# Seven weight tiles' low parts and the pooled channels' low parts, on GpSimd instead of VectorE, during the attention of a hybrid decoder layer

## The chip, the cores and the metric

The kernel runs on one core of a Trainium2 chip. The engines are named as in the profile: PE is TensorE, DVE is VectorE, ACT is ScalarE, POOL is GpSimd, SP is the engine that issues most DMAs. The metric is the device time of one execution in microseconds. The kernel before takes 2540.4 us, the median of three runs from 2538.5 to 2542.72.

## The reference

One layer of a decoder trunk is computed for a prompt of 2048 tokens and for a group of 64 sample tokens, all in float32, with a model width of 1024. Cut to what matters here:

```
h = rmsnorm(x, g_mix);  proj = h @ w_in                 # 1024 -> 512 (q) + 128 (k) + 128 (v) + 512 (u)
p = softmax(q.k / 8 - slope * distance, with a sink)    # 8 heads, window of 128 keys back
attn_o = p @ v
for g, w in enumerate((2, 4, 8, 16)):                   # four groups of 128 channels of u
    d[g] = mean of the last w rows of u[g] - u[g]
pool_o = d @ w_pool * pool_scale
x = x + concat(attn_o, pool_o) @ w_out
x = x + cross_attention(rmsnorm(x), 256 memory tokens) @ w_co
x = x + relu(rmsnorm(x) @ w_up)**2 @ w_down             # hidden 4096
y = rmsnorm(x)
```

The 64 sample tokens have key, value and pooling caches of their own. Caches that the step leaves behind are outputs too.

## The kernel before

**Precision.** PE multiplies a rounded float format (fp32r), so each float32 operand is held as two tiles: `hi`, the value rounded to that format, and `lo`, the rounded rest, `x - hi`. Each product is then three matmuls: hi by hi, hi by lo, lo by hi (`mm3`, and the loop of `dense`, L352 to L354). Making the pair takes a cast to `hi` on ACT and then a subtraction to `lo` on DVE. For weights this is `split`: L118 is the cast of a tile of 128x1024, L119 the subtraction. For activations taken from PSUM it is `rnd` (L97 and L98, with a scale L100 and L101).

**Tokens and weights.** The tokens go through in three superblocks of two token blocks each: 384 and 384, then 256 and 320 (256 of the prompt and the 64 sample tokens), then 384 and 384. The weights are streamed from device memory again for each superblock. The object `S` is this stream: a list of items, each a DMA into one of six `f` tiles and then `split` into two `w` tiles. A pump keeps up to five items ready ahead of their use.

**The stretch around the change.** The input projection has ten column tiles, "in" 0 to 9. Tiles 0 to 5 are keys, values and queries. Tiles 6, 8, 7, 9, in this order, are the four groups of `u`. When the first tiles are through, `mix` interleaves two generators: one runs the projection of the `u` tiles (its three matmuls are L352 to L354), the other runs the attention units. A unit is one block of 128 queries for one of two key heads, in stages: scores on PE (L754) with their maximum on DVE (L755), exponentials on ACT (L766), scaling of the probabilities (L776: one of four heads on DVE, three on POOL), transposes on PE (L785) with `rnd` on ACT and DVE, then the product with v (L802, L803) and its evacuation (L806, L807).

When a `u` tile of one token block is complete, ACT copies it to `uext` (L643), POOL saves or restores the 15 carried columns (L642, L647) and `pool_mix` builds the window sum on POOL by doubling (L672: one addition for window 2, up to four for window 16; for the sample tokens L701). After a delay `pool_fin` turns it into the pooled difference on DVE (L686, sample L706), corrects the first 16 columns on POOL in the first superblock only (L689, L690), casts it to `hi` on ACT (L709) and subtracts to `lo` on DVE (L710). Its output is the second half of the input of the output projection, "wo" 0 to 7, which follows directly in `dense` with L352 to L354 and adds to x in `add_evac` (L970).

**What sets the order.** Python runs the generators and so emits the instructions; a scheduler of the tile framework then reorders them per engine by its own costs, and each engine runs its list strictly in that order. An instruction that waits holds up all behind it on its engine.

Of the kernel before, what the change touches and what calls it, by code (L numbers as in the profile page):

```python
# [12 lines left out]
ALU = mybir.AluOpType  # L13
# [38 lines left out]
def kernel(ctx: ExitStack, tc: tile.TileContext, io, nW=12, nF=6, nT=10):  # L52
    nc = tc.nc
    pool = ctx.enter_context(tc.tile_pool(name="sb", bufs=1))
# [13 lines left out]
    wo_s = drp.tile([8, P, 512], F32, name="wo_s", tag="wo_s")  # L68
# [23 lines left out]
    def f32(ap):  # L92
        return ap.bitcast(F32)
# [9 lines left out]
    def k4(t, n=NB):  # L103
        return t[:, 0:4 * NB].rearrange("p (k n) -> p k n", n=NB)[:, :, 0:n]
# [8 lines left out]
            nc.tensor.matmul(ps, Wh(k), Hl(k), start=False, stop=False)  # L113
            nc.tensor.matmul(ps, Wl(k), Hh(k), start=False, stop=final and i == last)  # L114

    def split(r):
        th, tl = WS.get(), WS.get()
        nc.scalar.copy(th[:], r[:, 0:1024])  # L118
        nc.vector.tensor_tensor(tl[:], r[:, 0:1024], f32(th[:]), ALU.subtract)  # L119
        return th, tl  # L120

    class FB:
# [2 lines left out]
    class Stream:  # L125
# [3 lines left out]
            self.resW = 0  # L129
            self.resF = 0  # L130

        def add(self, key, *raw):
            def fn():
                r = FS.get()
                w = 1024 // len(raw)
                for i, src in enumerate(raw):
                    nc.sync.dma_start(r[:, w * i:w * i + w], src)
                t = split(r)
                FS.put(r)
                return t  # L140

            self.items.append((key, 2, 1, fn))
# [20 lines left out]
    S = Stream()  # L163
# [43 lines left out]
        S.add(("co", c), io["wco"][c])  # L207
    for s in range(3):
        for c in CIN:
            S.add(("in", s, c), io["win"][c])  # L210
            if s == 0 and c in (0, 1):
                for g in range(2):
                    S.add(("wop", 2 * c + g), io["wop"][2 * c + g])
        for c in range(8):
            S.add(("wo", s, c), io["woa"][c], wo_s[c])
        for hf in range(2):
            for kp in range(4):
                S.add(("A", s, hf, kp), a_s[hf, kp])
        for c in BO:
            S.add(("B", s, c), b_s[c])  # L220
        for p in range(NP):
            add_up(s, p)
            pl = (p - 1, p) if p == NP - 1 or s == 1 and p % 2 else () if p == NP - 2 or s == 1 else (p,)
            for t in range(2):
                for i in pl:
                    S.add(("dn", s, i, t), io["wdn"][2 * i + t])
# [332 lines left out]
    def superblock(s, blks, nxt):  # L559
# [120 lines left out]
        def pool_fin(g, bl, src, prev):  # L680
            w = POOLW[g]
            n = bl.np
            ucur = uext[:, g, bl.off + 15:bl.off + 15 + n]
            assert len(dpool.free) == 4
            dt = TS.get()
            nc.vector.scalar_tensor_tensor(dt[:, 0:n], src[:, 0:n], 1.0 / w, ucur, ALU.mult, ALU.subtract)  # L686
            if bl.t0 == 0:
                rc = cst[:, C_RC + 16 * g:C_RC + 16 * g + 16]
                nc.gpsimd.tensor_tensor(dt[:, 0:16], src[:, 0:16], rc, ALU.mult)  # L689
                nc.gpsimd.tensor_tensor(dt[:, 0:16], dt[:, 0:16], ucur[:, 0:16], ALU.subtract)  # L690
            TS.put(prev)
            if bl.ns:
                src = us[:, g, :, 16 - w:23]
                L = 8 + w - 1
                step = 1
                prev = None
                while step < w:
                    t = TS.get()
                    L -= step
                    tv = t[:, 0:8 * L].rearrange("p (b t) -> p b t", t=L)  # L700
                    nc.gpsimd.tensor_tensor(tv, src[:, :, step:step + L], src[:, :, 0:L], ALU.add)  # L701
                    if prev is not None:
                        TS.put(prev)
                    prev, src = t, tv
                    step *= 2
                nc.vector.scalar_tensor_tensor(dt[:, n:n + 64].rearrange("p (b t) -> p b t", t=8), src, 1.0 / w, us[:, g, :, 15:23], ALU.mult, ALU.subtract)  # L706
                TS.put(prev)
            hi, lo = k4(bl.d[0], bl.n)[:, g, :], k4(bl.d[1], bl.n)[:, g, :]
            nc.scalar.copy(hi, dt[:, 0:bl.n])  # L709
            nc.vector.tensor_tensor(lo, dt[:, 0:bl.n], f32(hi), ALU.subtract)  # L710
            TS.put(dt)
            if bl.ns and g == CIN[-1] - 6:
                t = FS.get()
                nc.scalar.copy(t[:, 0:480].rearrange("p (x t) -> p x t", t=15), X0[:, 4 * uw:4 * uw + 736].rearrange("p (x t) -> p x t", t=23)[:, :, 8:23])
                nc.sync.dma_start(io["pools"], t[:, 0:480])
                FS.put(t)
# [566 lines left out]
        def up(p, H=None):  # L1283
# [25 lines left out]
            p6 = prod(wb, (512, 512), "T2")  # L1309
            WS.put(*wb)  # L1310
            r2 = add(TS.get(), p6, r1)
            r4 = add(TS.get(), p5, r2, False)
            w22, *wd = S.next(("up", s, p, 2))
            add(r4, prod(wd, (512, 512), "B22"), r4)
            relu2(H, 1, 0, r4)
            flush()
# [233 lines left out]
```

## Time and profile before

| what | value |
|---|---|
| median of three runs | 2540.4 us |
| profiled execution, its own time | 2537.34 us |
| its span | 2535.3 us |
| PE busy | 98% |
| DVE busy | 73% |
| ACT busy | 43% |
| POOL busy | 7% |

The span runs from the first to the last instruction that the profiler recorded; 2.04 us of the execution's own time lie around it. Where a row has a time and a duration, both are in microseconds from the span's start. A group's row gives the line, engine, operation and tiles, the count after `x`, the busy time, the mean of one in nanoseconds, and then the idle time just ahead of these instructions with what ended it. In a row of the timeline the brackets give the idle time before it and what released it.

### The profile page before, as it was taken

Reading aid. Unit: us, or ns where it says so; the run is one execution under the profiler, and the core shown is the slowest. Engines: PE = TensorE matmul, PEld = TensorE weight load, DVE = VectorE, ACT = ScalarE, POOL = GpSimd, SP = SyncE. Lnnn points to the kernel's source line nnn. Section 1 sums busy time; section 2 is a strip of 40 time slices with the busy share of each in tenths; the row PEclk is TensorE's granted clock in tenths of the full one; section 3 lists DMA queues with packets and bytes.
Section 4 is the critical chain, followed back from the end, with each engine's and each line's share of the span. In section 5 each row is a group of like instructions: output and inputs, shape, how many; then the busy total and the mean of one; then the engine's idle time right before and its main releaser. Section 6 shows DMA issues by size and latency. Waiting matters only on the chain.

```text
span 2535.3 us, 38897 instructions
## 1 busy us (share of the span) xinstructions
PE 2483.3 (98%) x15199; PEld 2368.2 (93%) x15199; DVE 1858.8 (73%) x3687; ACT 1098.6 (43%) x2131; POOL 172.5 (7%) x282
## 2 busy tenths in 40 slices
PE   9899999999999999999999999999999999999998
PEld 9798989999999998996899999989998999999997
DVE  8568537877777788863787877898745877777775
ACT  7666334433333344752544334457534433333332
POOL 0015010000000001411000000003301000000000
PEclk9999999999999999999999999999999999999999
DMA  8833211222222125246522222240412121222211
GB/s 289 270 122 104 92 34 59 67 67 67 67 67 67 61 81 154 82 148 237 212 92 100 76 92 92 88 143 26 142 42 68 42 67 67 67 67 68 67 58 50
DMA packets 92540, 244.73 MB, mean 97 GB/s; under 512 B 16772, under 2 KB 31556, under 8 KB 91204
## 3 DMA queue, kind: packets, MB, share of 16 engines
q1 hardware_dynamic: 92356, 242.25, 28.8%
q8 instruction: 119, 1.95, 0.3%
q14 instruction: 65, 0.53, 0.1%
HBM read 219.53 MB, written 22.69 MB: 96 GB/s over the span
## 4 chain that ended last, share of the span: by engine, by line
PE 78%; DVE 4%; ACT 1%; DMA 1%; POOL 1%; issue 0%; POOLq 0%; DVEq 0%; ACTq 0%
PE mm L112 11%; PE mm L113 11%; PE mm L114 11%; PE aux L112 9%; PE aux L113 9%; PE aux L114 9%; PE mm L352 5%; PE mm L354 5%; PE mm L353 5%; PE aux L754 1%; PE aux L785 1%; DVE x L1371 1%; PE aux L1082 0%; ACT w L118 0%; DVE t L300 0%
## 5 line engine op out<-in xcount | busy, mean ns | idle before, releaser
L118 ACT CAST w<-f 128x1024 fp32r<-128x1024 f32 x378 | 395.6, 1050 | 731.5 <-PE mm L114 366.6
L119 DVE TENSOR_TENSOR w<-f,w 128x1024 fp32r<-128x1024 f32 x378 | 460.4, 1222 | 185.6 <-PE aux L113 98.3
L113 PE MATMUL mm<-act,w 128*128 128x384 f32 (+2 forms) x1728 | 552.8, 320 | 0.0
L114 PE MATMUL mm<-act,w 128*128 128x384 f32 (+2 forms) x1728 | 550.7, 319 | 0.8 <-DVE w L119 0.8
L112 PE MATMUL mm<-act,w 128*128 128x384 f32 (+2 forms) x1728 | 537.9, 321 | 3.4 <-DVE t L459 2.2
L112 PE MATMUL aux<-act,w 128*128 128x384 f32 (+1 forms) x1344 | 432.4, 322 | 3.6 <-DVE t L264 2.7
L114 PE MATMUL aux<-act,w 128*128 128x384 f32 (+1 forms) x1344 | 432.1, 322 | 0.0
L113 PE MATMUL aux<-act,w 128*128 128x384 f32 (+1 forms) x1344 | 431.9, 321 | 0.0
L352 PE MATMUL mm<-act,w 128*128 128x384 f32 (+2 forms) x1248 | 408.7, 328 | 7.3 <-DVE x L1350 2.9
L354 PE MATMUL mm<-act,w 128*128 128x384 f32 (+2 forms) x1248 | 405.1, 325 | 3.2 <-DVE w L119 3.1
L353 PE MATMUL mm<-act,w 128*128 128x384 f32 (+2 forms) x1248 | 405.9, 325 | 1.6 <-DVE act L302 1.2
L1350 DVE TENSOR_TENSOR x<-mm,x 128x384 f32<-128x384 f32 (+3 forms) x672 | 313.8, 493 | 125.8 <-PE mm L114 124.1
L112 PEld LDWEIGHTS mm<-act,w 128*128 128x128 f32 x1728 | 322.8, 189 | 13.3 <-ACT act L1279 7.0
L113 PEld LDWEIGHTS mm<-act,w 128*128 128x128 f32 x1728 | 326.5, 189 | 5.4 <-DVE act L1280 3.8
L114 PEld LDWEIGHTS mm<-act,w 128*128 128x128 f32 x1728 | 326.1, 189 | 2.0 <-DVE w L119 1.0
L112 PEld LDWEIGHTS aux<-act,w 128*128 128x128 f32 x1344 | 252.7, 188 | 4.8 <-DVE t L264 3.2
L114 PEld LDWEIGHTS aux<-act,w 128*128 128x128 f32 x1344 | 253.4, 189 | 0.3
L113 PEld LDWEIGHTS aux<-act,w 128*128 128x128 f32 x1344 | 253.5, 189 | 0.0
L352 PEld LDWEIGHTS mm<-act,w 128*128 128x128 f32 x1248 | 238.8, 191 | 13.7 <-issue 3.9
L353 PEld LDWEIGHTS mm<-act,w 128*128 128x128 f32 x1248 | 238.7, 191 | 7.4 <-DVE act L302 2.8
L354 PEld LDWEIGHTS mm<-act,w 128*128 128x128 f32 x1248 | 238.5, 191 | 5.6 <-DVE w L119 4.9
L1292 DVE TENSOR_TENSOR t<-aux,t 128x384 f32<-128x384 f32 (+1 forms) x336 | 169.4, 517 | 24.4 <-PE aux L114 18.7
(227 smaller groups left out, 3001.2 us busy)
## 6 DMA issues: line engine op xcount, KB each, us to landing
f<-in_wup SPq DMA_DIRECT2D x96, 512.0 KB, 3.7
f<-in_wdn SPq DMA_DIRECT2D x96, 512.0 KB, 3.7
f<-in_win SPq DMA_DIRECT2D x30, 512.0 KB, 3.8
f<-a_s SPq DMA_DIRECT2D x24, 512.0 KB, 3.8
f<-b_s SPq DMA_DIRECT2D x24, 512.0 KB, 4.4
x<-in_x SPq DMA_DIRECT2D x6, 1536.0 KB, 7.4
f<-in_wco SPq DMA_DIRECT2D x16, 512.0 KB, 5.3
f<-in_cmk SPq DMA_DIRECT2D x16, 512.0 KB, 4.4
```

The source lines that it names most:

```text
L112: nc.tensor.matmul(ps, Wh(k), Hh(k), start=first and i == 0, stop=False)
L113: nc.tensor.matmul(ps, Wh(k), Hl(k), start=False, stop=False)
L114: nc.tensor.matmul(ps, Wl(k), Hh(k), start=False, stop=final and i == last)
L118: nc.scalar.copy(th[:], r[:, 0:1024])
L119: nc.vector.tensor_tensor(tl[:], r[:, 0:1024], f32(th[:]), ALU.subtract)
L352: nc.tensor.matmul(ps[:, 0:n], w8(th)[:, k, :], hi(b, k), start=k == 0, stop=False)
L353: nc.tensor.matmul(ps[:, 0:n], w8(th)[:, k, :], lo(b, k), start=False, stop=False)
L354: nc.tensor.matmul(ps[:, 0:n], w8(tl)[:, k, :], hi(b, k), start=False, stop=k == 7)
L754: nc.tensor.matmul(o, q[:, j, c0:c0 + P], kz[kv][hl][:, so + k0:so + 256], start=hl == 0, stop=hl == 1)
L785: nc.tensor.transpose(ps[:, P * j:P * j + P], u.Lv[:, j, P * kb:P * kb + P], ident[:])
L1292: nc.vector.tensor_tensor(t[:, 0:hn], ps[:, 0:hn], r[:, 0:hn], ALU.add)
L1350: nc.vector.tensor_tensor(x, ps[:, o:o + n], x, ALU.add)
```

## The change

`split` gets a flag. With it, the subtraction runs on POOL in two halves of 512 columns instead of once on DVE. The flag is set for the input tiles 6 to 9 and for the wo tiles 0, 1 and 2 of each superblock. In `pool_fin` the subtraction to `lo` moves from DVE to POOL as it is. The values computed are the same. Lines behind `split` are numbered 4 higher after the change: the halves are L121, the subtraction that stays on DVE is L123, L672 becomes L676, L686 becomes L690, L710 becomes L714.

```diff
-    def split(r):
+    def split(r, pool=False):
         th, tl = WS.get(), WS.get()
         nc.scalar.copy(th[:], r[:, 0:1024])
-        nc.vector.tensor_tensor(tl[:], r[:, 0:1024], f32(th[:]), ALU.subtract)
+        if pool:
+            for o in (slice(0, 512), slice(512, 1024)):
+                nc.gpsimd.tensor_tensor(tl[:, o], r[:, o], f32(th[:, o]), ALU.subtract)
+        else:
+            nc.vector.tensor_tensor(tl[:], r[:, 0:1024], f32(th[:]), ALU.subtract)
         return th, tl
...
-        def add(self, key, *raw):
+        def add(self, key, *raw, pool=False):
...
-                t = split(r)
+                t = split(r, pool)
...
         for c in CIN:
-            S.add(("in", s, c), io["win"][c])
+            S.add(("in", s, c), io["win"][c], pool=c >= 6)
...
         for c in range(8):
-            S.add(("wo", s, c), io["woa"][c], wo_s[c])
+            S.add(("wo", s, c), io["woa"][c], wo_s[c], pool=c < 3)
...
             nc.scalar.copy(hi, dt[:, 0:bl.n])
-            nc.vector.tensor_tensor(lo, dt[:, 0:bl.n], f32(hi), ALU.subtract)
+            nc.gpsimd.tensor_tensor(lo, dt[:, 0:bl.n], f32(hi), ALU.subtract)
```

Since the scheduler orders each engine, the change also moves instructions that the diff doesn't touch, on all engines, but only inside the three stretches. Three places follow. The names are tiles: `w` and `f` weight tiles and their raw data, `t` scratch tiles, `act` activation tiles, `x_107` the tile that holds `u`.

POOL at the end of the first superblock's attention, before: the last two groups' window sums of the first token block, then the small corrections.

```order
L672 TENSOR_TENSOR t_106<-x_107 128x386
L672 TENSOR_TENSOR t_101<-t_106 128x384
L672 TENSOR_TENSOR t_97<-x_107 128x398
L672 TENSOR_TENSOR t_98<-t_97 128x396
L672 TENSOR_TENSOR t_100<-t_98 128x392
L672 TENSOR_TENSOR t_102<-t_100 128x384
L689 TENSOR_TENSOR t_97<-t_102,cst 128x16
L690 TENSOR_TENSOR t_97<-t_97,x_107 128x16
```

The same place after:

```order
L676 TENSOR_TENSOR t_101<-t_106 128x384
L121 TENSOR_TENSOR w_81<-f_93,w_87 128x512 x2
L121 TENSOR_TENSOR w_86<-f_94,w_88 128x512 x2
L714 TENSOR_TENSOR act_74<-t_99,act_73 128x384
L676 TENSOR_TENSOR t_97<-x_107 128x398
L676 TENSOR_TENSOR t_98<-t_97 128x396
L676 TENSOR_TENSOR t_100<-t_98 128x392
L121 TENSOR_TENSOR w_82<-f_95,w_83 128x512
L676 TENSOR_TENSOR t_102<-t_100 128x384
L121 TENSOR_TENSOR w_82<-f_95,w_83 128x512
L693 TENSOR_TENSOR t_97<-t_102,cst 128x16
L694 TENSOR_TENSOR t_97<-t_97,x_107 128x16
```

The halves of wo tiles 0 and 1 and one pooled low part stand ahead of the last group's four sums, and the two halves of wo tile 2 between them and the corrections.

DVE at the end of the second superblock's attention, before: the last pooled differences, the low parts of wo tiles (into `w_85`, `w_86` and others) and the pooled low parts.

```order
L686 SCALAR_TENSOR_TENSOR t_102<-t_101,x_107 128x256
L119 TENSOR_TENSOR w_85<-f_91,w_87 128x1024
L710 TENSOR_TENSOR act_74<-t_102,act_73 128x256
L119 TENSOR_TENSOR w_82<-f_93,w_89 128x1024
L807 TENSOR_TENSOR cp_145<-mm_109,cp_145 64x512
L686 SCALAR_TENSOR_TENSOR t_99<-t_103,x_107 128x256
L706 SCALAR_TENSOR_TENSOR t_99<-t_98,x_107 128x64
L119 TENSOR_TENSOR w_86<-f_92,w_79 128x1024
```

POOL at that place after, from the second wo tile on:

```order
L121 TENSOR_TENSOR w_85<-f_91,w_87 128x512 x2
L714 TENSOR_TENSOR act_74<-t_102,act_73 128x256
L651 COPY ucar<-x_107 128x15
L676 TENSOR_TENSOR t_98<-x_107 128x270
L705 TENSOR_TENSOR t_105<-x_107 128x176
L676 TENSOR_TENSOR t_104<-t_98 128x268
L705 TENSOR_TENSOR t_97<-t_105 128x160
L676 TENSOR_TENSOR t_106<-t_104 128x264
L705 TENSOR_TENSOR t_100<-t_97 128x128
L676 TENSOR_TENSOR t_103<-t_106 128x256
L705 TENSOR_TENSOR t_98<-t_100 128x64
L121 TENSOR_TENSOR w_86<-f_92,w_79 128x512 x2
```

The low part into `w_86`, that of wo tile 2, stood behind two pooled differences on DVE and stands behind the last chain of window sums on POOL now.

## The prediction

> **What bounds the kernel now.** I read the page's busy times first, then the table of stretches, then what TensorE (PE) waits for in them.
>
> ```profile
> PE 2483.3 (98%) x15199; PEld 2368.2 (93%) x15199; DVE 1858.8 (73%) x3687; ACT 1098.6 (43%) x2131; POOL 172.5 (7%) x282
> L119 DVE TENSOR_TENSOR w<-f,w 128x1024 fp32r<-128x1024 f32 x378 | 460.4, 1222 | 185.6 <-PE aux L113 98.3 <-ACT w L118 51.4 <-ACT t L1277 16.2
> ```
>
> PE is busy 98% of the span. VectorE (DVE) has a quarter of its time free over the whole, so its mean says nothing for the change; what counts is whether it holds PE up where the change acts. Those are three stretches, one per superblock, in which the attention runs between pieces of the last input projections: 140 to 256, 1020 to 1084 and 1712 to 1812 us.
>
> ```profile
> core 0: us, PE busy (x) PEld busy (x) DVE busy (x) ACT busy (x) POOL busy (x), PEclk, DMA share, GB/s
> 140.00:256.00 116.00, 112.35 (x673) 105.28 (x672) 89.61 (x247) 76.53 (x198) 44.38 (x68) 1.00 0.30 98
> 1020.00:1084.00 64.00, 60.63 (x412) 55.97 (x413) 54.75 (x166) 47.00 (x135) 33.32 (x59) 0.95 0.24 76
> 1712.00:1812.00 100.00, 98.37 (x599) 91.90 (x598) 85.13 (x240) 72.35 (x192) 44.08 (x60) 1.00 0.23 75
> ```
>
> Each row gives busy time with counts per engine, then the granted clock. Two things are in it. DVE is at 77%, 86% and 85% here, GpSimd (POOL) at 38%, 52% and 44%. And PE's idle time, all there is to win without a change of clock, is 116 - 112.35 = 3.65, then 3.37 and 1.63: 8.65 us, 0.34% of the kernel. What PE waited for, as "total, times, longest", per stretch (the second list starts at 1006):
>
> ```profile
> PE mm L352 <- ACT act L709: 1.6, 1, 1.6
> PE aux L754 <- DVE st L755: 1.4, 4, 0.7
> PE aux L785 <- DVE vt L98: 0.3, 1, 0.3
> ```
> ```profile
> PE mm L354 <- DVE w L119: 2.2, 1, 2.2
> PE mm L802 <- ACT w L97: 0.5, 1, 0.5
> PE aux L754 <- DVE st L755: 0.4, 1, 0.4
> ```
> ```profile
> PE aux L754 <- DVE st L755: 1.1, 2, 0.9
> PE aux L785 <- POOL x L776: 0.2, 1, 0.2
> ```
>
> Two single stalls, 1.6 and 2.2, make up 3.8 of the 8.65: both stand at the end of a stretch, where the output projection (wo) starts. The score matmuls' waits for L755 on DVE are 1.4 + 0.4 + 1.1 = 2.9 us, and a vt wait adds 0.3. With those under 0.2 each that the lists leave out (8.65 - 7.7 listed = about 1), DVE's own queue costs PE some 4.2 us.
>
> That is a little short, as a matmul record overlaps the next and hides some of each stall:
>
> ```profile
> 248.76 0.33 PE L352 MATMUL mm<-act,w 128*128 128x384 f32 x1
> 248.94 0.33 PE L353 MATMUL mm<-act,w 128*128 128x384 f32 x1
> ```
>
> Each is 0.33 long but the next starts 0.18 later, so a stall is shown some 0.15 too short. For the 8 listed waits on L755 and vt (4 + 1 + 1 + 2) that is about 1 us more, so **5 us** is DVE's share in the middle of the stretches.
>
> **The change, part by part.** Per superblock, seven low-part subtractions of 1.222 us leave DVE (8.6 us), and eight pooled-channel ones of 0.6 us (4.8): 13.4 of the 89.6 us of the first row, 15%.
>
> ```profile
> L710 DVE TENSOR_TENSOR act<-t,act 128x384 fp32r<-128x384 f32 x8 | 4.8, 605 | 2.2 <-ACT act L709 2.1
> ```
>
> On POOL there arrive 14 halves of 128x512 and the same eight. The trace has no two-input subtraction of 512 columns there; the nearest rows are the window sums of L672.
>
> ```profile
> L672 POOL TENSOR_TENSOR t<-t 128x384 f32<-128x384 f32 x12 | 10.9, 912 | 0.9
> L672 POOL TENSOR_TENSOR t<-x 128x256 f32<-128x256 f32 x2 | 1.2, 612 | 14.4 <-ACT x L643 14.4
> L672 POOL TENSOR_TENSOR t<-x 128x398 f32<-128x398 f32 x4 | 8.6, 2146 | 4.6 <-ACT x L643 4.6
> 236.01 0.82 POOL L672 TENSOR_TENSOR t<-t 128x384 f32<-128x384 f32 x1
> ```
>
> From 256 to 384 undisturbed columns the time goes from 612 to 820 ns, 1.63 ns a column; 512 then take 0.82 + 128 x 1.63 ns = 1.03 us. From the mean 912 it would be 1.12. I take 1.04 and keep 1.2 as the upper bound. 14 x 1.04 + 8 x 0.82 = 21 us more on POOL, against 13.4 saved on DVE: 44 becomes 65 of 116, 33 becomes about 52 of 64 (its last groups are 256 and 320 wide), 44 becomes 65 of 100. POOL does not become the fullest engine.
>
> The mean of 2146 for 398 columns, against 0.82 for 384, is the other thing that decides. Here is its longest case:
>
> ```profile
> 237.95 1.21 DVE L119 TENSOR_TENSOR w<-f,w 128x1024 fp32r<-128x1024 f32 x1
> 239.08 0.54 DVE L710 TENSOR_TENSOR act<-t,act 128x384 fp32r<-128x384 f32 x1
> 239.55 2.35 DVE L119 TENSOR_TENSOR w<-f,w 128x1024 fp32r<-128x1024 f32 x2
> 238.76 3.85 POOL L672 TENSOR_TENSOR t<-x 128x398 f32<-128x398 f32 x1 [1.92 <-ACT x L643]
> 242.69 2.86 POOL L672 TENSOR_TENSOR t<-t 128x396 f32<-128x396 f32 x3
> ```
>
> While DVE runs subtractions that read two operands from on-chip memory back to back, POOL's sum does not get on: it begins at 238.76 and ends at 242.61, 0.7 us after DVE's last at 241.90; the three behind it take 0.95 each. So one side holds up the other. The Trainium skill, page "SBUF — State Buffer", section "Who interferes with whom", says so too: GpSimd and a VectorE instruction with two such inputs take one port pair as a lock, and the later is fully blocked for the whole instruction; these rows agree. By that rule and the caution in "Perfetto Trace Analysis", section "Optimizing Scalar/DVE Operations", that moving work between the two might not help, the 21 us now taken on POOL are 21 us in which such DVE work is shut out, and the gain taken below would be nothing: a sum of +1.6, 2542.
>
> From the rows alone the same follows in part: what leaves DVE was itself such a subtraction, and DVE's other two-input work (L98 from the copies, L686) now meets more POOL work. In the trace POOL loses mostly: L710's mean is 605 ns against 0.54 undisturbed, 12%. Bounds for the relief: all 5 us back at best, and below nothing, -3, if DVE is held longer than it saves. I take **-3 us**, over half, since all DVE work of L755 reads its scores from PSUM, and what stood ahead of it was often the 1.22 us of L119.
>
> **The end of the first stretch.** POOL's order puts two tiles' halves and a low part ahead of the sums quoted above:
>
> ```profile
> 245.58 0.56 DVE L686 SCALAR_TENSOR_TENSOR t<-t,x 128x384 f32<-128x384 f32 x1 [2.96 <-POOL t L672]
> 247.15 0.51 ACT L709 CAST act<-t 128x384 fp32r<-128x384 f32 x1 [3.87 <-POOL t L690]
> 247.69 0.56 DVE L710 TENSOR_TENSOR act<-t,act 128x384 fp32r<-128x384 f32 x1 [0.96 <-ACT act L709]
> 247.71 0.45 PE L352 MATMUL mm<-act,w 128*128 128x384 f32 x1 [1.57 <-ACT act L709]
> ```
>
> POOL is free from 236.83. Four halves (4.2) and one low part (0.8) from then end near 241.8; then the four sums at their undisturbed price and one half between them (0.85 + 2 x 0.9 + 1.04 + 0.9 = 4.6) end at 246.4, where before they ended at 245.55. Another half stands before the two small POOL fixes of 16 columns, hidden in part behind L686. So the cast comes 0.8 to 1.1 later, and its low part, now on POOL for 0.83 in place of 0.56, up to 1.4 later. PE stood 1.57 for it and now stands about **+1.0 us** longer (0.5 to 2).
>
> **The end of the second.** PE waits 2.2 us for the third wo tile's low part, which stood in DVE's queue behind an L686 that waited for POOL:
>
> ```profile
> 1080.93 0.53 DVE L686 SCALAR_TENSOR_TENSOR t<-t,x 128x256 f32<-128x256 f32 x1 [3.04 <-POOL t L672]
> 1081.52 1.21 DVE L119 TENSOR_TENSOR w<-f,w 128x1024 fp32r<-128x1024 f32 x1
> 1075.46 1.77 POOL L647 COPY ucar<-x 128x15 f32<-128x15 f32 x1 [1.84 <-ACT x L643]
> 1080.86 0.31 POOL L701 TENSOR_TENSOR t<-t 128x64 f32<-128x64 f32 x1
> 1082.79 0.39 PE L354 MATMUL mm<-act,w 128*128 128x256 f32 x1 [2.22 <-DVE w L119]
> ```
>
> That wait could go; it doesn't, because the two halves now stand on POOL behind the whole chain that L686 waited for (it ends at 1081.17), and the second tile's halves stand ahead of that chain. 1081.17 + 0.2 for what is ahead + 2 x 1.04 = 1083.4, against 1082.73 before: **+0.5 us** (0 to 1.2).
>
> **The end of the third** has no listed wait, so a delay of 1 us is partly covered by wo's matmuls: **+0.1** (0 to 1). The rest costs nothing as long as its cover holds: a split tile is ready well before its matmuls, POOL's scaling L776 kept PE waiting only 0.2, and the scheduler's new interleaving of PE's own work (about as many changes between projection and attention pieces) has no price of its own. If the cover of L776 went, by halves ahead of it in POOL's queue, its transposes would wait up to 1 us each time.
>
> **The sum.** -3 + 1.0 + 0.5 + 0.1 = -1.4 against the profiled execution's own 2537.34 (2.04 of it outside the span of 2535.3), thus 2535.9. That execution stands 3.1 below the median of 2540.4; so the runs should show about **2539 us**.
>
> **The clock** can turn a stall into more, or less:
>
> ```profile
> 118.00:128.00 10.00, 6.38 (x22) 5.18 (x23) 6.16 (x12) 7.52 (x15) 0.00 (x0) 0.83 0.60 191
> 386.00:396.00 10.00, 8.12 (x47) 7.57 (x46) 5.00 (x10) 3.52 (x9) 1.81 (x2) 1.00 0.25 73
> 1016.00:1028.00 12.00, 12.00 (x74) 11.84 (x75) 4.65 (x22) 2.11 (x9) 0.61 (x1) 0.72 0.34 112
> 1080.00:1090.00 10.00, 7.78 (x58) 7.58 (x58) 7.03 (x13) 3.55 (x9) 1.51 (x4) 1.00 0.79 297
> 1944.00:1954.00 10.00, 8.13 (x38) 7.58 (x37) 4.35 (x8) 2.25 (x6) 1.81 (x2) 0.83 0.14 49
> ```
>
> 1.9 us of idle time went unpunished at 386 and cost 10 x 0.17 = 1.7 us of clock at 1944; 2.2 at 1080 cost nothing; 3.6 at 118 cost 1.7; the loss before 1028 is 12 x 0.28 = 3.4. A shifted stall may draw or escape 1.7 to 3.4 us. "TensorE: Matmul & The Clock Gate" in the Trainium skill puts this down to free-running windows of activity, which would make it a matter of where the stall falls; no row here shows the windows themselves.
>
> **The rivals.**
>
> (a) DVE was pacing the attention. Then the 5 us go, and half-hidden ones with them, up to the idle time that is not at the ends, 8.65 - 3.8 = 4.9, plus 0.15 hidden in each of some twenty small stalls, 3; -8 with the ends' lower bounds of +0.5 is -7.5: **2533**. For it: DVE at 85%. Against: the same rows show PE losing only 1.6% in the third stretch at that load.
>
> (b) POOL's queue becomes the bound of the ends. One mechanism: in order, the halves wait for their ACT cast, and the sums of the last group wait behind them; it decides from about 3 us of stall, where the clock falls (the 118 row). That needs 1.4 more at the first end and 0.8 more at the second, both near my upper bounds. Price: 1.4 + 0.8, two clock losses of 1.7 to 3.4, and most of the relief lost to the same blocking: +5.6 to +9, so +7: **2547**. For it: 3.85 us for one sum. Against: the three L119 that blocked it leave DVE.
>
> (c) Nothing but the order changes: the relief and the later ends are both under 1 us, 2540; this ends within the forecast's own span.
>
> That the moved work is not done on POOL is excluded by the order of instructions.
>
> **How the numbers follow.** Two tenths of a percent, 5.1 us, is about what a measurement here can tell from no change. Forecast with (c): 0.43, own range 2536 to 2544. (a) 0.33; part of its chance is the clock losing fewer windows than before. (b) 0.24. Below 2535.3 lies (a), above 2545.5 (b). The range that holds 8 in 10 cuts the outer third of each: 2531 to 2547.
>
> **What would show it.** In the first stretch DVE should fall to about 77 us busy, POOL rise to about 65, halves at 1.0 to 1.2 us each. The L755 waits should fall from 2.9 towards 1; the wait for L709's cast (there with the new line number) should grow from 1.6 to about 2.6, and the one at 1082.79 should name POOL and be 2.5 to 3. It is wrong if halves take over 1.5 us, if PE's idle time in the middle of the stretches doesn't fall, or if a clock row below 1.00 appears at 244 to 254 or 1080 to 1090.

## The result: 1.09% slower

The changed kernel takes 2567.67 us (median of four runs, 2564.75 to 2570.16) against 2541.56 for the kernel before beside it: a ratio of 1.0109, with a 95% interval of 1.0093 to 1.0125. The forecast of no change, 2539 us, was wrong, and so was its range of 2531 to 2547. The loss, 26.1 us, lies on the side of rival (b), at nearly four times its price.

The page of the changed kernel, its busy times, one group and two groups of POOL:

```profile
PE 2494.7 (97%) x15199; PEld 2377.4 (93%) x15199; DVE 1845.6 (72%) x3642; ACT 1099.5 (43%) x2131; POOL 237.5 (9%) x348
L356 PE MATMUL mm<-act,w 128*128 128x384 f32 (+2 forms) x1248 | 411.7, 330 | 18.1 <-ACT act L713 12.1
```
```profile
L121 POOL TENSOR_TENSOR w<-f,w 128x512 fp32r<-128x512 f32 x42 | 57.1, 1381 | 10.1 <-ACT w L118 10.1
L714 POOL TENSOR_TENSOR act<-t,act 128x384 fp32r<-128x384 f32 x16 | 16.3, 1017 | 11.3 <-ACT act L713 11.3
```

The span is 2568.4, 33.1 longer than before. PE's busy time grew by 2494.7 - 2483.3 = 11.4 (the same matmuls, part of them at a lower clock, as shown below), so its idle time grew by the other 21.7. What PE waits for, over the whole span:

```profile
PE aux L758 <- DVE st L759: 14.2, 15, 3.2
PE mm L356 <- ACT act L713: 12.1, 3, 5.7
...
PE mm L357 <- POOL act L714: 1.8, 3, 1.0
PE mm L358 <- POOL w L121: 1.4, 1, 1.4
```

The first two before:

```profile
PE aux L754 <- DVE st L755: 2.9, 7, 0.9
PE mm L352 <- ACT act L709: 1.6, 1, 1.6
```

So the relief of DVE did not shorten the waits for the score maxima; they grew by 11.3, and the waits for the pooled channels' cast by 10.5. DVE itself was relieved of little: the moved instructions had taken about 40 us there (21 x 1.22 for the weight tiles and 14.1 for the pooled low parts), but its busy time fell only from 1858.8 to 1845.6. The instructions that stayed took over 20 us longer, 8.1 of it the pooled differences (24 took 12.7 us before and 20.8 after).

**Where it happens.** Measured in each profile from the start of a superblock's first score matmul to the start of its last addition of the output projection, the three stretches took 157.5, 108.0 and 156.6 us before and 169.2, 113.8 and 167.8 after: +28.7 of the 33.1. Inside them PE stood idle for 8.6 us before and 30.8 after; its busy time there, 413.5 and 420.1, makes the other 6.6. The sum of the three stretches, 422.1 before and 450.8 after, is used below for the experiments, since what lies outside moves by several us from one profile to the next whatever the kernel (2105 to 2118 over all profiles of this study). Two profiles of one and the same kernel (the last group's sums on DVE, below) have sums of 419.4 and 421.3, so a difference of 2 us says nothing.

The row that the prediction should have looked for is busy time in the last part of a stretch, not in the whole. First the kernel before, then after:

```profile
core 0: us, PE busy (x) PEld busy (x) DVE busy (x) ACT busy (x) POOL busy (x), PEclk, DMA share, GB/s
235.00:255.00 20.00, 18.28 (x102) 17.52 (x101) 10.92 (x16) 8.13 (x13) 13.51 (x13) 1.00 0.56 200
```
```profile
215.00:235.00 20.00, 16.38 (x96) 15.17 (x95) 14.95 (x42) 14.33 (x39) 14.92 (x22) 0.91 0.22 67
235.00:255.00 20.00, 18.74 (x107) 17.84 (x105) 9.41 (x11) 11.21 (x18) 18.94 (x21) 1.00 0.52 184
255.00:275.00 20.00, 15.11 (x76) 14.71 (x77) 6.17 (x9) 4.30 (x8) 9.72 (x12) 0.83 0.39 132
1090.00:1110.00 20.00, 16.55 (x109) 15.63 (x108) 11.77 (x16) 9.68 (x19) 15.94 (x20) 0.91 0.59 213
1820.00:1840.00 20.00, 14.26 (x70) 13.36 (x69) 9.36 (x9) 8.19 (x12) 18.27 (x18) 0.84 0.58 199
```

POOL was busy 13.5 of 20 us at 235 before, 68% already, and is busy 18.9 of 20 there and 18.3 at 1820 now: it is full, while DVE works less than half the time. Since the ends come later after the change, the fairer comparison counts back from the end of PE's stall: in the 20 us up to there POOL was busy 13.9 and 15.0 us at the first two ends before, and is busy 18.6, 19.8 and 18.8 at the three ends after. The clock column shows the second loss: 0.91 and 0.83 where the waits of 3.2 and 5.7 us stand, 20 x (0.09 + 0.17) = 5.2 us in the first stretch. That is an upper bound, as PE stands still for part of it: from 256.8 to 259.4 the granted clock is 0.50 and PE is busy 0.00 us.

**How POOL's queue reaches the score matmuls.** The timeline of POOL, DVE and PE at the 3.2 us wait (a row's `x2` merges two in a row):

```profile
218.97 2.55 POOL L121 TENSOR_TENSOR w<-f,w 128x512 fp32r<-128x512 f32 x2
221.47 1.01 POOL L714 TENSOR_TENSOR act<-t,act 128x384 fp32r<-128x384 f32 x1
222.44 0.19 POOL L651 COPY ucar<-x 128x15 f32<-128x15 f32 x1
222.59 0.83 POOL L676 TENSOR_TENSOR t<-x 128x390 f32<-128x390 f32 x1
223.49 1.74 POOL L676 TENSOR_TENSOR t<-t 128x388 f32<-128x388 f32 x2
```
```profile
225.26 0.56 DVE L690 SCALAR_TENSOR_TENSOR t<-t,x 128x384 f32<-128x384 f32 x1 [3.66 <-POOL t L676]
225.74 0.48 DVE L759 CUSTOM_DVE_ANT_0 x<-aux,cst,vec 128x256 f32<-128x256 f32 x1
```
```profile
226.28 0.79 PE L758 MATMUL aux<-w,act 128*128 128x256 f32 x2 [3.25 <-DVE st L759]
```

Two halves and a pooled low part, 3.5 us, stand ahead of three window sums. DVE's L690 is the next in DVE's list, needs the last sum and stands idle 3.66 us; the score maximum behind it could run, as PE had done its scores before it fell idle, but DVE keeps its order too; PE needs that maximum's buffer. Each engine keeps its own order, so a late sum on the emptiest engine stops the fullest one.

**The end of the first stretch**, POOL first:

```profile
242.44 0.82 POOL L676 TENSOR_TENSOR t<-x 128x386 f32<-128x386 f32 x1
...
244.13 6.36 POOL L121 TENSOR_TENSOR w<-f,w 128x512 fp32r<-128x512 f32 x4
250.44 1.02 POOL L714 TENSOR_TENSOR act<-t,act 128x384 fp32r<-128x384 f32 x1
251.41 0.86 POOL L676 TENSOR_TENSOR t<-x 128x398 f32<-128x398 f32 x1
...
255.28 0.99 POOL L676 TENSOR_TENSOR t<-t 128x384 f32<-128x384 f32 x1
256.23 1.26 POOL L121 TENSOR_TENSOR w<-f,w 128x512 fp32r<-128x512 f32 x1
```
```profile
256.31 1.60 DVE L690 SCALAR_TENSOR_TENSOR t<-t,x 128x384 f32<-128x384 f32 x1 [6.19 <-POOL t L676]
```
```profile
258.93 0.51 ACT L713 CAST act<-t 128x384 fp32r<-128x384 f32 x1 [8.15 <-POOL t L694]
```
```profile
259.49 0.69 PE L356 MATMUL mm<-act,w 128*128 128x384 f32 x1 [5.75 <-ACT act L713]
```

The four halves take 6.36 us, 1.59 each where 1.04 was forecast, and the last group's sums begin at 251.41 and not near 242. L690 itself takes 1.60 here in place of 0.56: it starts 0.08 after a half on POOL, which ends at 257.49, and ends 0.42 after that.

### The profile page after: what moved, and what is told of

It reads as the page before. It is cut to its first block, busy times and chain, and to the rows that moved or that the text cites. A ratio compares the mean times of both kernels' runs of the same rounds, so it can differ in the third digit from the quotient of the medians.

```text
span 2568.4 us, 38906 instructions
## 1 busy us (share of the span) xinstructions
PE 2494.7 (97%) x15199; PEld 2377.4 (93%) x15199; DVE 1845.6 (72%) x3642; ACT 1099.5 (43%) x2131; POOL 237.5 (9%) x348
## 4 chain that ended last, share of the span: by engine, by line
PE 75%; DVE 4%; ACT 2%; POOL 1%; DMA 1%; issue 1%; POOLq 0%; SPq 0%; DVEq 0%; ACTq 0%
PE mm L112 11%; PE mm L113 11%; PE mm L114 10%; PE aux L112 9%; PE aux L113 9%; PE aux L114 9%; PE mm L358 5%; PE mm L357 5%; PE mm L356 5%; DVE x L1375 1%; ACT x L770 1%; PE aux L758 1%; POOL w L121 1%; POOL t L676 0%; DVE t L304 0%
## 5 line engine op out<-in xcount | busy, mean ns | idle before, releaser
L123 DVE TENSOR_TENSOR w<-f,w 128x1024 fp32r<-128x1024 f32 x357 | 438.3, 1231 | 190.1 <-PE aux L113 98.2
L356 PE MATMUL mm<-act,w 128*128 128x384 f32 (+2 forms) x1248 | 411.7, 330 | 18.1 <-ACT act L713 12.1
L112 PEld LDWEIGHTS mm<-act,w 128*128 128x128 f32 x1728 | 322.9, 189 | 14.2 <-ACT act L1283 7.0
```

The source lines that it names most:

```text
L112: nc.tensor.matmul(ps, Wh(k), Hh(k), start=first and i == 0, stop=False)
L356: nc.tensor.matmul(ps[:, 0:n], w8(th)[:, k, :], hi(b, k), start=k == 0, stop=False)
```

## The experiments

All ratios are against the kernel before, run beside it on the same chip, with 95% intervals. The stretch sum is that of one profile (422.1 before, 450.8 for the change). The expectations speak of two theories: by the queue theory the loss comes from POOL's ordered list, by the port theory from instructions of POOL and DVE that block each other. In the diffs `-` is the changed kernel, where nothing else is said.

### The three parts of the change, each alone

Only the input tiles:

```diff
-            S.add(("wo", s, c), io["woa"][c], wo_s[c], pool=c < 3)
+            S.add(("wo", s, c), io["woa"][c], wo_s[c], pool=False)
...
-            nc.gpsimd.tensor_tensor(lo, dt[:, 0:bl.n], f32(hi), ALU.subtract)
+            nc.vector.tensor_tensor(lo, dt[:, 0:bl.n], f32(hi), ALU.subtract)
```

> Only the halves of the four input tiles 6 to 9 of each superblock are on POOL; the wo tiles' and the pooled channels' low parts stay on DVE. The queue theory (POOL's strictly ordered list gets longer, its window sums come later, and the pooled difference on DVE that waits for a sum holds up the score maxima behind it, so PE waits in L758): the long L758 waits of the change (14.2 us in all) come back in part, 4 to 8 us, since two halves of 1.3 us stood ahead of a window sum there; the cast waits at the ends of the first and third stretch stay under 3 us each; time +4 to +9 us against before, about 2547. The port theory (POOL's longer two-input work blocks DVE while it runs): the loss goes with the time moved, 42 halves and 24 pooled parts took 80 us on POOL in the change and cost 26 us, so these 24 halves (31 us) cost about 10 us, spread over many short waits. If only the scheduler's other order counted, the size would not follow the amount moved.

Measured: 2545.15 us, 1.0023 (1.0014 to 1.0033); stretch sum 430.9, +8.8. The time, +4.2 us, is at the low end of the queue theory's +4 to +9 and far from the 10 of the port theory. The score waits are 9.6 us in all (2.9 before, 14.2 for the change) and the cast waits 1.8, as the queue theory had it.

Only the wo tiles (`pool=False` for the input tiles, the pooled low parts on DVE):

> Only the halves of wo tiles 0, 1 and 2 of each superblock are on POOL. The queue theory: the loss is at the ends of the stretches, since these halves stand ahead of the last window sums: the cast waits of L713 are 3 to 5 us at the first and third end in place of 1.6 and none, each with a clock loss of 1.7 to 3.4 us; L758 waits stay near the 2.9 us of before; time +8 to +12 us, about 2551. The port theory: 18 halves (23 us of POOL time) cost about 7 to 8 us, spread over the stretches and not gathered at the ends.

Measured: 2547.16 us, 1.0029 (1.0017 to 1.0041); stretch sum 433.1, +11.0. Its waits answer the forecast of the queue theory at the ends:

```profile
PE mm L356 <- ACT act L713: 5.8, 2, 4.2
...
PE aux L758 <- DVE st L759: 3.0, 7, 0.9
```

The loss is gathered at the ends, and the score waits are those of before. The time, +6.3 us, stays below the +8 to +12 of the queue theory: the stall at the third end was 1.6 us and not 3 to 5.

Only the pooled low parts (`pool=False` for all weight tiles):

> Only the 24 pooled-channel low parts are on POOL; all weight tiles stay on DVE. The queue theory: each stands 1.0 us on POOL ahead of the next group's window sums, and waits for its cast on ACT first; L758 waits grow by 2 to 5 us, the ends by about 1 us each; time +3 to +7 us, about 2546. The port theory: 23 us of POOL time cost about 7 us. If the three parts alone add up to much less than the 26 us of the whole, POOL's free time absorbs each alone and the loss is one of a queue that fills.

Measured: 2542.74 us, 1.0009 (0.9999 to 1.0019), not told apart from before; stretch sum 427.5, +5.4, in the profile of the slowest of its ten runs. Both theories had forecast more (+3 to +7, and 7), and the score waits, which the queue theory had growing, are 1.5 us in place of 2.9; the cast waits grew to 3.5.

The three alone cost 0.23 + 0.29 + 0.09 = 0.61%, the whole 1.09%. By the profiles' stretch sums they are nearly additive, 8.8 + 11.0 + 5.4 = 25.2 against 28.7. The medians say that the loss grows faster than the work moved; the stretch sums don't settle it.

### The pooled difference issued later

```diff
-            late.append([2, lambda: pool_fin(g, bl, src, prev)])
+            late.append([4, lambda: pool_fin(g, bl, src, prev)])
```

> The whole change, but the pooled difference is issued 4 ticks of the attention's stages after its window sums in place of 2, so DVE meets it later and POOL has longer to be done with the sums. The queue theory: DVE no longer stands idle for the sums with score maxima behind it: DVE's waits for L676 in the middle of the stretches fall from up to 3.7 us to under 1, L758 waits of PE fall from 14.2 us to under 5, time falls by 7 to 12 us against the change (to about 2558); the ends, where nothing is left to put between, stay as they are or grow by 1 us. The port theory: POOL and DVE do the same work, so L758 waits stay above 10 us and the time stays within 3 us of the change.

Measured: 2566.8 us, 1.0108 (1.0093 to 1.0123): nothing gained. The order of DVE's instructions tells why. The scheduler put L690 back to nearly the same place: in the first and the third stretch one L690 of eight stands two instructions later than in the change and the others stand as they did; in the second a few more moved. So this run decides between no theories, though its time is the one that the port theory forecast. It does show that on this kernel such a delay is no means to move an instruction.

### DVE does not wait for the sums

```diff
-            nc.vector.scalar_tensor_tensor(dt[:, 0:n], src[:, 0:n], 1.0 / w, ucur, ALU.mult, ALU.subtract)
+            nc.vector.scalar_tensor_tensor(dt[:, 0:n], ucur, 1.0 / w, ucur, ALU.mult, ALU.subtract)
```

> The whole change, but the pooled difference on DVE is computed from the channels alone and does not read the window sum (the pooling is thereby left out of the result; all sums and all moved low parts are still done on POOL). So DVE never waits for POOL's sums, while every instruction on POOL and nearly every one on DVE stays. The chain theory (most of the loss is DVE's L690 waiting for a sum that comes late on POOL, with score maxima behind it, and at the ends the cast that waits for the same L690): DVE's wait for L676, 40 us in the change, is gone, PE's L758 waits fall from 14.2 to under 5 us, the cast waits from 12.1 to under 3, time about 2545. The port theory (POOL's two-input work blocks DVE's, whose instructions got longer): L758 waits stay above 9 us and the time above 2555.

Measured: 2561.82 us, 1.0079 (1.0062 to 1.0097); stretch sum 446.3, +24.2. The chain theory's 2545 missed by 17 us. Of the port theory's two signs the time held (above 2555) and the score waits did not (7.3 us, forecast above 9). PE's waits in this run:

```profile
PE aux L758 <- DVE st L759: 7.3, 12, 1.6
PE mm L358 <- POOL w L121: 6.0, 4, 3.4
PE mm L357 <- POOL act L714: 5.5, 3, 4.3
...
PE mm L356 <- ACT act L713: 3.3, 1, 3.3
```

The score waits fell from 14.2 to 7.3, so the path by L690 is real, but taking it away brought back only some 5 us of the 26 (+21.3 us against before in place of +26.1; by the stretch sums 4.5). The ends did not come back: PE now waits for the halves and the low parts themselves, 6.0 and 5.5 us. POOL's list is as long as before and PE waits for whatever comes last in it.

### The same POOL time without reading

```diff
-            for o in (slice(0, 512), slice(512, 1024)):
-                nc.gpsimd.tensor_tensor(tl[:, o], r[:, o], f32(th[:, o]), ALU.subtract)
+            for o, m in ((slice(0, 512), 2), (slice(512, 1024), 3)):
+                for _ in range(m):
+                    nc.gpsimd.memset(f32(tl[:, o]), 0.0)
```

> The whole change, but each weight tile's two subtractions on POOL are replaced by five fills of 512 columns with zeros (2 and 3 for the halves; the weight's low part is thereby left out of the result). At 0.5 us each they take about the 2.6 us of the two halves, but read nothing from on-chip memory and wait for no cast. The queue theory (POOL's time in its list is what counts, whatever it does): time within 6 us of the change, 2561 to 2573, cast waits of 4 us or more at the first and third end. The port theory (what hurts is that a POOL instruction with two inputs and a DVE instruction with two exclude each other): DVE's instructions get back their durations of before (L123 and L98 with no slow cases beside the fills), time 2545 to 2552.

Measured: 2555.06 us, 1.0057 (1.0042 to 1.0072), between the two; stretch sum 438.3, +16.2. A fill took 525 ns, 105 of them 53.1 us against the halves' 57.1. Since fills wait for no cast, they can run earlier than the halves, so a second run made them wait, by one more line ahead of them:

```diff
+            nc.scalar.copy(tl[:, 0:1024:512], r[:, 0:1024:512])
```

> As the run with fills of zeros in place of the weights' subtractions on POOL, but each tile's fills must first wait for ACT (a two-column copy into the low tile right behind the cast), as the subtractions did, so that POOL's list is nearly that of the change and the fills can't slip ahead. POOL then has the change's queue, time and waits; only the reading of two operands is gone. The low part is left out of the result. If POOL's queue alone makes the loss: 2562 to 2568, as the change. If mutual blocking makes the part by which the fills were better (2555 against 2567): again 2553 to 2557, with DVE's instructions as long as in the run with fills. I expect the second.

Measured: 2558.56 us, 1.0077 (1.0064 to 1.009); stretch sum 448.0, +25.9. That is between the two expectations and not what I expected. With about the change's POOL time (232.6 us in all, 237.5 for the change), but no operand read for the weights on POOL, 0.77 of the 1.09% remain (0.7 of the loss; by the stretch sums 0.9). So POOL's time in its list makes most of it. The rest, 3 us by the stretch sums and 7 by the medians, goes with the reading, but the run does not separate it cleanly: POOL's order is not that of the change, as the scheduler set the last tiles' fills in between the window sums, and PE waits 7.5 us for fills here and only 2.2 for the cast. DVE's group rows for 140 to 270 show the blocking by halves directly, first the kernel before, then after, then this run:

```profile
L686 DVE SCALAR_TENSOR_TENSOR t<-t,x 128x384 f32<-128x384 f32 x8 | 4.7, 593 | 7.1 <-POOL t L672 7.1
```
```profile
L690 DVE SCALAR_TENSOR_TENSOR t<-t,x 128x384 f32<-128x384 f32 x8 | 6.6, 822 | 17.0 <-POOL t L676 17.0
```
```profile
L692 DVE SCALAR_TENSOR_TENSOR t<-t,x 128x384 f32<-128x384 f32 x8 | 4.4, 555 | 14.8 <-POOL t L678 14.8
```

The mean goes from 593 to 822 ns with the halves and back to 555 with fills; the idle time before it, the queue's part, stays: 7.1, 17.0, 14.8.

### One instruction in place of two halves

```diff
-            for o in (slice(0, 512), slice(512, 1024)):
-                nc.gpsimd.tensor_tensor(tl[:, o], r[:, o], f32(th[:, o]), ALU.subtract)
+            nc.gpsimd.tensor_tensor(tl[:], r[:, 0:1024], f32(th[:]), ALU.subtract)
```

> The change with each moved weight tile's low part as one POOL instruction of 1024 columns in place of two of 512. The queue theory: the same POOL time less some fixed cost (two halves of 1.26 against one of about 2.4), but no sum can come between the halves: time within 4 us of the change. The port theory: a DVE instruction that meets it is blocked up to 2.4 us in place of 1.3, so DVE's lengthened instructions (L690 1.6, L775 0.9) get longer still and the time is 5 us or more above the change.

Measured: 2566.62 us, 1.0107 (1.0092 to 1.0122), as the change. The cut into halves neither helps nor harms, as the queue theory had it.

### The relief of DVE alone

```diff
-            for o in (slice(0, 512), slice(512, 1024)):
-                nc.gpsimd.tensor_tensor(tl[:, o], r[:, o], f32(th[:, o]), ALU.subtract)
+            nc.vector.tensor_tensor(tl[:, 0:64], r[:, 0:64], f32(th[:, 0:64]), ALU.subtract)
...
-            nc.gpsimd.tensor_tensor(lo, dt[:, 0:bl.n], f32(hi), ALU.subtract)
+            nc.vector.memset(f32(lo), 0.0)
```

> What leaving DVE is worth by itself: of each moved weight tile's low part only 64 of the 1024 columns are computed, on DVE, and the pooled low part is filled with zeros on DVE; nothing moves to POOL (the rest of these low parts is thereby left out of the result). About 11 us of DVE time per superblock are gone and POOL does what it did before. The prediction's term was -3 us with bounds 0 to -5 for the waits, and less at the ends (stalls of 1.6 and 2.2 us, the second of which stood behind a moved subtraction). If DVE paces the attention: 5 to 9 us faster than before. If relief is worth nothing: within 2 us of before. I expect -3 to -5 us, about 2537.

Measured: 2531.26 us, 0.9966 (0.9953 to 0.9979): -8.4 us. The stretch sum is 417.3, -4.8. So the work that left DVE does hold the kernel up, but not where the prediction looked for it. The score waits, to which its -3 us belonged, are longer than the 2.9 of before:

```profile
PE aux L757 <- DVE st L758: 6.4, 7, 1.9
```

With less to do, DVE reaches the pooled difference sooner and stands there for POOL's sum, 2.55 us ahead of 219.73 in this run, with score maxima behind it; before the change DVE did not wait for POOL between 208 and 222. What is gone are the two stalls at the ends, 1.6 and 2.2 us. Where the rest of the 8.4 us comes from is not shown. The change does not show this gain, because what POOL takes back is some 26 + 8 = 34 us.

### The sums the other way

The whole change, with the window sums on DVE:

```diff
-                nc.gpsimd.tensor_tensor(t[:, 0:L], src[:, step:step + L], src[:, 0:L], ALU.add)
+                nc.vector.tensor_tensor(t[:, 0:L], src[:, step:step + L], src[:, 0:L], ALU.add)
```

> The whole change, and all window sums of the prompt tokens go the other way, from POOL to DVE. POOL keeps the 42 halves, the 24 pooled low parts and the scaling; about 17 us of sums per superblock leave its queue and come to DVE as about 20 x 0.55 = 11 us, so DVE is about as full as before the change. The queue theory (POOL full in the last 20 us of each stretch, with the sums the ends wait for behind halves): the ends come back, cast waits of 12.1 us fall under 3, time 2541 to 2550. The port theory (two-input work of both engines at once): as much of it as before runs on both, time above 2555.

Measured: 2560.03 us, 1.0082 (1.0067 to 1.0097); stretch sum 443.6. The queue theory alone fails here: POOL lost its sums and 7 us came back, not 20. What holds it, on DVE and POOL at the first end:

```profile
244.68 1.38 DVE L676 TENSOR_TENSOR t<-x 128x398 f32<-128x398 f32 x1
246.17 1.48 DVE L676 TENSOR_TENSOR t<-t 128x396 f32<-128x396 f32 x1
247.68 0.69 DVE L811 TENSOR_TENSOR cp<-mm,cp 64x512 f32<-64x512 f32 x1
248.40 2.36 DVE L676 TENSOR_TENSOR t<-t 128x392 f32<-128x392 f32 x2
```
```profile
243.63 2.00 POOL L714 TENSOR_TENSOR act<-t,act 128x384 fp32r<-128x384 f32 x1
245.59 4.76 POOL L121 TENSOR_TENSOR w<-f,w 128x512 fp32r<-128x512 f32 x3
```

Three of these four sums take 1.4 to 1.5 us on DVE and one 0.8, where most of the same run take about 0.55; three halves take 1.59 each in place of 1.26. The two engines take turns, each waiting for the other's instruction. That is the rule cited in the prediction from the Trainium skill, "SBUF — State Buffer", section "Who interferes with whom", and these rows agree with it. So moving the sums from one to the other did not keep them out of each other's way. PE still waits 9.9 us for the cast, 12.1 with the change.

### Only the first tile

```diff
-            S.add(("in", s, c), io["win"][c], pool=c >= 6)
+            S.add(("in", s, c), io["win"][c], pool=c == 6)
```

(wo tiles and pooled low parts on DVE.)

> Only the two halves of input tile 6, the first of the seven, run on POOL in each superblock; they come early in the stretch, when POOL is busy 5 to 20% and has no window sum to do yet. The queue theory: nothing waits behind them, so the time is within 2 us of before (2539 to 2542) with at most 1 us gain from DVE's relief. The port theory: a loss in proportion, 6 of 42 halves and of 80 us of POOL time, about 2.6 us.

Measured: 2540.17 us, 1.0000 (0.999 to 1.0009). Where POOL is nearly idle, the move costs nothing and gains nothing that can be seen. The 2.6 us of the port theory lie just outside the interval.

### The opposite move on the kernel before

The last group's sums, of window 16, on DVE, all else as before the change (`-` is the kernel before):

```diff
-                nc.gpsimd.tensor_tensor(t[:, 0:L], src[:, step:step + L], src[:, 0:L], ALU.add)
+                (nc.vector if g == CIN[-1] - 6 else nc.gpsimd).tensor_tensor(t[:, 0:L], src[:, step:step + L], src[:, 0:L], ALU.add)
```

> The kernel before with the opposite move: the four window sums of the last group of channels (window 16), which the ends of the stretches wait for, run on DVE in place of POOL; nothing else. On DVE a sum of 384 columns should take about 0.55 us (as L710 does), four of them 2.2, against 6.7 us on POOL at the first end. The queue theory: DVE stands idle there for POOL's sums in any case (3 to 4 us each time), so the stall of 1.6 us at the first end and that of 2.2 at the second go; time 2 to 6 us faster than before, about 2537. The port theory says the same for POOL but puts 24 x 0.55 = 13 us on DVE: no gain, within 2 us of before.

> The same kernel as the run with the last group's sums on DVE (0.9991 of before, interval 0.9982 to 1.0001), with more rounds, beside the run with two groups: 2536 to 2539, a gain of 2 to 3 us by the stall of 2.2 us at the end of the second stretch that it took away. If it was chance: within 1 us of before.

Measured: 2538.08 us, 0.9991 (0.9982 to 1.0001), and with more runs 2537.06 us, 0.9995 (0.9986 to 1.0004): not told apart from before. The second stretch was 2.5 us shorter in both profiles (105.4 and 105.6 against 108.0), but that is too little for the whole to show. The stall at the second end went, as expected; that at the first did not (1.9 us).

The last two groups, windows 4 and 16:

> The kernel before with the window sums of the last two groups (windows 4 and 16 here, the last two in order) on DVE in place of POOL. If both engines share one way to memory for two-input work, it is the time on it that counts: a sum costs 0.85 to 0.95 us there from POOL and 0.55 from DVE, so 18 us less of it in all against 12 for the last group alone; a gain of 2 to 5 us, 2535 to 2538. If DVE's own fullness (85%) counts: no gain or a loss of 2 us against the last group alone.

Measured: 2535.76 us, 0.9984 (0.9975 to 0.9993): 4 us faster than the kernel before, as the first of the two expectations had it. It is little, and the profile does not show where it comes from: the stretch sum is 421.9, as before.

All four groups:

> The kernel before with the prompt's window sums of all four groups on DVE; POOL keeps the scaling and the small copies. If the shared time of two-input work is what counts and DVE's fullness does not, this goes on from the two groups (2536, 0.9984 of before): about 20 us less of POOL time per superblock than before, 11 more on DVE; 2533 to 2536. If DVE, 85% full before in the middle stretches, becomes the limit, score maxima come later, the L754 waits grow from 2.9 to over 5 us, and the time is 2538 or more.

Measured: 2549.77 us, 1.0039 (1.0025 to 1.0053): slower again, though not by L754 as expected, whose wait fell to 1.8 us. The waits that grew over the whole span:

```profile
PE aux L785 <- POOL x L776: 5.4, 5, 1.6
...
PE mm L803 <- DVE w L98: 2.8, 3, 1.4
```

They are waits for POOL's scaling and for a low part on DVE. DVE's fullness can be the cause of both, as the scaling in turn waits for DVE's L772; that DVE and POOL block each other is not ruled out as another.

So the division of before was within 0.2% of the best of those tried, and both directions cost: too much on POOL 1.1%, too much on DVE 0.4%.

## Why the prediction was wrong

**The terms of the sum.** Forecast were -3 for the relief and +1.0, +0.5 and +0.1 for the ends. Measured were +11.3 for the score waits in place of the relief, +4.2, +1.2 and +5.3 for the ends, and 6.6 us of longer matmuls, which the sum had at nothing; together this is close to the 28.7 of the stretches. The side was missed because two steps failed: that POOL stays far from full, and that its list can be timed from where it stood before.

**What bounds the kernel.** Right that DVE was the engine PE waits for in the middle of the stretches, and that these waits are small. Wrong in the step "POOL does not become the fullest engine". It was made from the mean of the stretch (65 of 116 us, and POOL was indeed busy for 66.4 from 140 to 270), though the caution against means stood at the start for DVE. In the last 20 us of the first stretch POOL went from 13.9 to 18.6 and was the fullest engine of all, with 14.3 for PE and 9.1 for DVE.

**The price of a half.** Forecast 1.04, at most 1.2, from sums that write plain float32. Measured 1.26 at the shortest (as in the last POOL row at the first end), 1.38 in the mean. The pooled low part took 1.01, forecast 0.82. Together (57.1 + 16.3 + 4.0 + 2.9, the last two the 320 and 256 column forms) / 3 = 26.8 us per superblock, forecast 21.

**The relief.** Forecast -3 at the score waits, bounds -5 to +3. Alone it is worth -8.4 over the whole kernel, but the profile shows the gain at the ends and not at these waits, which grew by 3.5; in the change they grew by 11.3. DVE was to fall from 89.6 to about 77 us in the first stretch and fell to 83.9 (140 to 270), since what stayed on it took longer. The sentence "the rest costs nothing as long as its cover holds" named L776 as the cover at risk. The one that went was another: DVE's own wait for POOL's sums at L686, which the quoted rows showed at 2.96 and 3.04 us at the ends, and whose place in the middle of DVE's list I did not price.

**The first end.** Forecast +1.0; the wait went from 1.57 to 5.75, though its bound was +2. The step that failed is "POOL is free from 236.83". I took POOL's timeline of before as the start and added what the change puts behind that moment, but four earlier tiles and five low parts had already made POOL late: the sums of the group ahead ran at 242.44 and not at 235. A delay on a queue has to be carried along from its first added instruction.

**The second and third ends.** Forecast +0.5 and +0.1; the working of the first of these, 1083.4 against 1082.73, gives 0.7. At the second, the named wait went to POOL as foreseen, smaller than before (1.4 after 2.2), but with the cast and a pooled low part at 1.0 us each besides. At the third, which had no wait, PE stood 5.3 us for the same reason as at the first: POOL's list ran from 1812 to 1834 without a gap, and DVE stood 6.18 us for a sum from it. The "delay of 1 us" there was the first end's error carried along.

**The clock.** The bounds of 1.7 to 3.4 us for a grown stall were right in kind. The rows that the prediction named, 244 to 254 and 1080 to 1090, stayed at 1.00, as the ends came later; but there were more such stalls than the two of rival (b), and the rows at 215, 255, 1090 and 1820 are all below 1.00. Of PE's 11.4 us of longer busy time 6.6 lie in the stretches; the rest lies outside, where the clock differs from one profile to the next.

**Rival (b)** named the mechanism, POOL's ordered queue ahead of the last sums, and the point from which the clock falls. Its price of +5.6 to +9 counted the ends alone, with my own upper bounds; the score waits behind DVE's L690 were in no rival. Rival (a) was half right: the work on DVE did cost 8 us, but not by the waits that (a) counted.

**What stays open.** How queue and blocking share the loss is known only roughly: the fills leave out the reading, but they need a small extra copy on ACT and come in another order on POOL, and by the medians 70%, by the stretch sums 90% of the loss remain. The score waits of 6.4 us without any added work on POOL show that part of their growth need not be POOL's longer list: a DVE that arrives sooner waits longer for the same sum. Whether the loss grows faster than the work moved isn't settled. Why two groups' sums on DVE gain 4 us isn't shown.

## What to carry to other kernels

Before work is moved to a lightly used engine, look at its busy share in the last 20 us before something is due, not over the stretch, and carry the added time along its list from the first added instruction. Then ask what the other engines' lists hold behind an instruction that waits for it: here a late sum on an engine that is busy 9% of the span stopped the score maxima on DVE, and through them PE. Between two engines that block each other, price the work by its time on the slower one: here 1.22 us on DVE became 2.55 us on POOL (two halves, the row at 218.97).

## What was not expected of the hardware

A subtraction on POOL that writes the rounded format takes longer than an addition of the same width that writes float32: 1.01 against 0.83 us for 384 columns, and 1.26 for 512. On DVE the two take about the same, 0.54 and 0.55. No run here separates the operation from the format. And the blocking reaches the smallest instructions: one on DVE of 128x4 that takes 0.17 us in the median took 0.95 beside a half on POOL.

```profile
220.59 0.95 DVE L763 TENSOR_SCALAR st<-st 128x4 f32<-128x4 f32 x1
221.46 0.15 DVE L764 TENSOR_TENSOR st<-vec,st 128x4 f32<-128x4 f32 x1
```

It ends at 221.54, just behind the half that ended at 221.52. A half is not needed for it: the longest of its kind in the kernel before took 0.80 beside a window sum, and one took 1.08 beside fills, which read nothing, in the run where they wait.
